# Sparse attention: queries and values projected ahead of the key rotation, and its low weight parts all made by GpSimd

## The chip, the core and the metric

One core of a Trainium2 chip runs the whole program in one launch. The metric is the device time of one execution in microseconds (us); less is better. In the views PE is TensorE (PEld its weight loads), DVE VectorE, ACT ScalarE, POOL GpSimd and SP the engine that issues the DMAs.

## What is computed

Two blocks over 512 tokens of width 1024, in float32. The first is a gated linear attention, a short convolution and a sliding-window attention, merged, with a gated feed-forward part behind. The second has two layers, and the change lies in each of them:

```python
for l in range(DEPTH_2):
    h = rmsnorm_2(x, norm_mix[l])
    proj = h @ w_in[l]
    aq, ak, av, iq, ik, iw, hq, hf, hi, hg, ga, gb = jnp.split(proj, split_points, axis=-1)
    aq = apply_rope(rmsnorm_2(aq.reshape(B, T, ATTN_HEADS, ATTN_HEAD_DIM), q_norm[l]), cos, sin)
    ak = apply_rope(rmsnorm_2(ak.reshape(B, T, ATTN_HEADS, ATTN_HEAD_DIM), k_norm[l]), cos, sin)
    ...
    y_attn = dsa_attention(aq, ak, av, iq, ik, iw)
```

`dsa_attention` scores every query against every earlier key with four small index heads, takes the 128 best keys of each query, and does the softmax of eight heads of width 64 over these alone. A gated recurrence (HGRN2) runs beside it; both are merged, and a feed-forward part ends the layer.

## The kernel before, in words

One Tile program: a scheduler gives each engine a queue, and each engine works through its queue in order. The scheduler follows the order in which the program is written, and a model of its own of when operations can run; `high_priority` sections (weight loads, evictions) go ahead of what is written before them.

**Weights.** Each float32 weight is used as a sum of a high and a low part, so that a product is three matmuls. `weights()` (L133 to L154) has SP load a block into `wraw` (three buffers); ACT casts the high part `whi` (L149), and an engine taken in turn from the list `self.lows` subtracts it to make the low part `wlo` (L152). `mixing()` (L101) sets that list to POOL, POOL, DVE; `feeding()` (L104) to DVE alone. There are three buffers of `whi` and of `wlo` each.

**Projections.** `project_tokens` (L156) gives tokens on partitions: for each of eight weight blocks and four groups of 128 tokens the matmuls L168 (`wlo`), L169 and L170, so 12 matmuls for each low part and 96 for a projection. `project` (L184) gives features on partitions, with L193 to L195.

**The sparse attention** is `dsa()` (L820), called by `second_mix` (L949). Its steps stand in the order of the string ORDER (L25): `x` projects the index inputs, `h` the gated values of the recurrence, `X` rotates the index inputs. `1`, `2`, `3` select the keys of the second to fourth group of 128 queries (over 256, 384 and 512 keys): sixteen rounds on DVE of a maximum (L878) and a replacement (L879), closed by L880. The first group needs no selection. `k`, `q`, `v` project keys, queries and values; for keys and queries ACT squares the result and DVE sums it (L805). `K` and `Q` rotate: `rotated()` (L810) makes a reciprocal root from those sums on DVE (L229 to L233), and for each of four groups of tokens `rope()` (L785) multiplies by the cosine table on POOL (L791) and by the sine table in two halves on DVE (L792, L793) and adds both on POOL (L794); then DVE scales by the root (L817) and PE transposes (L239). `a` to `d` attend, one group of queries each: scores on PE (L917), mask and maximum on DVE (L919), exponential on ACT (L921), transposes and products on PE (L925, L929). The projections of the recurrence and its heads, written behind `dsa()`, fill PE between these.

```python
        for c in ORDER:
            if c in steps:
                steps[c]()
            elif c in "123":
                select(int(c))
            else:
                attend("abcd".index(c))
```

Of the kernel before, what the change touches and what calls it, by code (L numbers as in the profile page):

```python
# [21 lines left out]
KD = 8  # L22
KF = 22
WARM = 12
ORDER = "xhX123kKqvQabcd"  # L25
EPS = 1e-6
NEG = -1e30
UNSEEN = -2e38
# [42 lines left out]
class Builder:  # L71
# [748 lines left out]
    def dsa(self, l, X):  # L820
# [62 lines left out]
        def inputs(j, name):  # L883
            got[name] = self.attention_inputs(A["w_tok"][l, j], X, name)
# [21 lines left out]
        def attend(i):  # L906
# [28 lines left out]
            for m in range(4):  # L935
# [3 lines left out]
                     q=lambda: inputs(1, "aq"), Q=rotate_queries, v=values, h=gated_values)  # L939
        for c in ORDER:  # L940
            if c in steps:
# [7 lines left out]
    def second_mix(self, l, X):  # L949
        nc, A = self.nc, self.A  # L950
        W = A["w_in2"][l]
        it = iter(range(W.shape[0]))
        proj = lambda: self.project(W[next(it)], X)

        with self.on("a"):
            yattn = self.dsa(l, X)
        if self.pending:
            self.settle()
        hv = self.hv
        yh = []  # L960
        for hd in range(4):
            F = self.scaled(proj(), "hf", self.i)
            k = self.i("hk")
            nc.scalar.activation(k, F, AF.Sigmoid, scale=-1.0)
            nc.scalar.activation(F, F, AF.Sigmoid)
            if l:
                nc.gpsimd.tensor_scalar(k, k, self.om[:, hd:hd + 1], None, op0=OP.mult)
                nc.vector.tensor_scalar(F, F, self.om[:, hd:hd + 1], self.lb[:, hd:hd + 1], op0=OP.mult, op1=OP.add)
            q = self.silu2(proj(), "hq")
            v = [a[:, hd * P:(hd + 1) * P] for a in hv]  # L970
            g = self.silu2(proj(), "hg")
            yh.append(self.hgrn_head(F, q, k, v, g, self.half[:, 4 + l:5 + l], "yh"))

        acc = self.merge(A["w_gate2"][l, 0], X, A["w_po"][l, 0], yattn, None, 2, False)
        return self.merge(A["w_gate2"][l, 1], X, A["w_po"][l, 1], yh, acc, 4, True)
# [121 lines left out]
```

## Time and profile before

| | us |
|---|---|
| three runs | 2609.94, 2606.26, 2607.33 |
| their median | 2607.33 |
| span of the profiled execution (no other time is given for it) | 2605.2 |
| PE busy | 2533.9 (97%) |
| DVE busy | 1355.5 (52%) |
| ACT busy | 1000.8 (38%) |
| POOL busy | 754.3 (29%) |

The span runs from the first to the last instruction of the profiled execution; it lies 0.08% below the median of the runs. Busy shares are means over the whole program. A timeline row gives start, duration, engine, line, operation, result and inputs, and in brackets the time that the engine was idle before it and the instruction that ended the wait. PEclk is the clock granted to TensorE as a share of the full 2.4 GHz; 0.50 is the lower level of 1.2 GHz.

### The profile page before, as it was taken

The numbers are of one execution on the slowest core, as the hardware profiler recorded it, in microseconds if no ns is written. First come the engines' busy times: TensorE is split into PE (matmuls) and PEld (weight loads), VectorE is DVE, ScalarE is ACT, GpSimd is POOL, SyncE is SP. The second block draws the span as 40 slices with busy tenths as digits, with TensorE's granted clock in tenths as the row PEclk, the third lists the DMA queues.
The fourth block names the chain that finished last, engine by engine and source line by source line (L and its number), as shares of the span: only waits on it lengthen the run. The fifth ranks groups of instructions, "written<-read, shape, count | busy, mean of one in ns | idle before, by whom it ended". The sixth has DMA issues, their size and how long they took to land.

```text
span 2605.2 us, 31523 instructions
## 1 busy us (share of the span) xinstructions
PE 2533.9 (97%) x11742; PEld 2040.0 (78%) x11742; DVE 1355.5 (52%) x2568; ACT 1000.8 (38%) x1813; POOL 754.3 (29%) x640
## 2 busy tenths in 40 slices
PE   9999999999999997999999999999799999999999
PEld 7777888788888865777878888887577787888887
DVE  4565322477774579675244444336967524444432
ACT  5543333444443333553343333334354433433321
POOL 4234334511101234443351111013545435211100
PEclk9999999999999999999999999999899999999999
DMA  3112222222222221111322222322110122222232
GB/s 135 57 51 81 93 94 93 101 97 96 97 94 90 90 73 65 42 41 51 99 96 94 97 95 94 96 88 81 65 49 33 45 94 97 97 97 97 95 101 87
DMA packets 67434, 217.66 MB, mean 84 GB/s; under 512 B 7744, under 2 KB 8640, under 8 KB 67280
## 3 DMA queue, kind: packets, MB, share of 16 engines
q1 hardware_dynamic: 67280, 215.65, 24.9%
q8 instruction: 92, 1.51, 0.2%
q14 instruction: 62, 0.51, 0.1%
HBM read 213.52 MB, written 2.10 MB: 83 GB/s over the span
## 4 chain that ended last, share of the span: by engine, by line
PE 83%; DVE 12%; issue 2%; POOL 2%; ACT 1%; DMA 0%; SPq 0%; DVEq 0%; POOLq 0%; ACTq 0%
PE mm L194 24%; PE mm L195 24%; PE mm L193 24%; PE at L917 1%; PE mm L169 1%; PE mm L168 1%; PE mm L170 1%; DVE score L879 1%; PE at L929 1%; DVE m L878 1%; DVE wlo L152 1%; PE at L239 1%; DVE hf L490 1%; DVE rope L792 1%; DVE rsq_w L232 1%
## 5 line engine op out<-in xcount | busy, mean ns | idle before, releaser
L149 ACT CAST whi<-wraw 128x512 fp32r<-128x512 f32 (+3 forms) x824 | 502.2, 610 | 1177.7 <-PE mm L195 992.1
L194 PE MATMUL mm<-xl,whi 128*128 128x512 f32 x1920 | 757.2, 394 | 0.0
L193 PE MATMUL mm<-xh,wlo 128*128 128x512 f32 x1920 | 756.8, 394 | 0.0
L195 PE MATMUL mm<-xh,whi 128*128 128x512 f32 x1920 | 755.5, 393 | 0.0
L152 DVE TENSOR_TENSOR wlo<-wraw,whi 128x512 fp32r<-128x512 f32 (+1 forms) x529 | 387.4, 732 | 457.9 <-ACT whi L149 455.2
L152 POOL TENSOR_TENSOR wlo<-wraw,whi 128x512 fp32r<-128x512 f32 (+2 forms) x295 | 383.6, 1301 | 767.0 <-ACT whi L149 747.1
L194 PEld LDWEIGHTS mm<-xl,whi 128*128 128x128 f32 x1920 | 361.7, 188 | 79.8 <-issue 7.5
L195 PEld LDWEIGHTS mm<-xh,whi 128*128 128x128 f32 x1920 | 361.6, 188 | 78.2 <-issue 5.6
L193 PEld LDWEIGHTS mm<-xh,wlo 128*128 128x128 f32 x1920 | 361.5, 188 | 76.6 <-issue 3.5
L193 PE MATMUL mm<-acth,wlo 128*128 128x512 f32 x528 | 208.6, 395 | 0.0
L195 PE MATMUL mm<-acth,whi 128*128 128x512 f32 x528 | 208.6, 395 | 0.0
L194 PE MATMUL mm<-actl,whi 128*128 128x512 f32 x528 | 208.6, 395 | 0.0
L725 POOL TENSOR_TENSOR fg<-fg,rstd 128x512 f32<-128x512 f32 x44 | 56.7, 1289 | 426.1 <-ACT fg L724 426.1
L168 PE MATMUL mm<-wlo,xh 128*128 128x512 f32 (+2 forms) x384 | 146.6, 382 | 20.0 <-POOL wlo L152 12.4
L170 PE MATMUL mm<-whi,xh 128*128 128x512 f32 (+2 forms) x384 | 144.5, 378 | 0.0
L169 PE MATMUL mm<-whi,xl 128*128 128x512 f32 (+2 forms) x384 | 144.2, 375 | 0.2 <-DVE xl L281 0.2
L202 DVE TENSOR_TENSOR gate<-mm,rstd 128x512 f32<-128x512 f32 x56 | 38.7, 691 | 169.3 <-PE mm L195 169.3
L270 POOL TENSOR_TENSOR acc<-acc,sq 128x512 f32<-128x512 f32 x39 | 58.7, 1506 | 205.9 <-ACT sq L267 204.9
L195 PEld LDWEIGHTS mm<-acth,whi 128*128 128x128 f32 x528 | 99.0, 187 | 24.3
L193 PEld LDWEIGHTS mm<-acth,wlo 128*128 128x128 f32 x528 | 99.0, 187 | 24.2
L194 PEld LDWEIGHTS mm<-actl,whi 128*128 128x128 f32 x528 | 99.0, 187 | 24.2
L168 PEld LDWEIGHTS mm<-wlo,xh 128*128 128x128 f32 x384 | 73.5, 191 | 40.7 <-POOL wlo L152 15.7
(347 smaller groups left out, 3288.3 us busy)
## 6 DMA issues: line engine op xcount, KB each, us to landing
wraw<-in_w_ffn_in SPq DMA_DIRECT2D x88, 512.0 KB, 3.2
wraw<-in_w_gate SPq DMA_DIRECT2D x56, 512.0 KB, 3.2
wraw<-in_w_in SPq DMA_DIRECT2D x52, 512.0 KB, 3.2
wraw<-in_w_up SPq DMA_DIRECT2D x44, 512.0 KB, 3.2
wraw<-in_w_tok SPq DMA_DIRECT2D x32, 512.0 KB, 3.2
wraw<-in_w_ffn_out SPq DMA_DIRECT2D x32, 512.0 KB, 3.5
wraw<-in_w_down SPq DMA_DIRECT2D x16, 512.0 KB, 3.5
wraw<-in_w_po SPq DMA_DIRECT2D x32, 256.0 KB, 2.6
```

The costliest lines, as they stand in the source:

```text
L149: nc.scalar.copy(wh, raw[:, k:k + m, :])
L152: eng.tensor_tensor(wl, raw[:, k:k + m, :], wh.bitcast(F32), op=OP.subtract)
L168: nc.tensor.matmul(ps[t][:, 0:w], xh, wl, start=i == 0, stop=False)
L169: nc.tensor.matmul(ps[t][:, 0:w], xl, wh, start=False, stop=False)
L170: nc.tensor.matmul(ps[t][:, 0:w], xh, wh, start=False, stop=i == KD - 1)
L193: nc.tensor.matmul(ps, wl, xh, start=i == 0, stop=False)
L194: nc.tensor.matmul(ps, wh, xl, start=False, stop=False)
L195: nc.tensor.matmul(ps, wh, xh, start=False, stop=i == n - 1)
L202: self.nc.vector.tensor_tensor(out, ps, other, op=OP.mult)
L232: nc.vector.scalar_tensor_tensor(w, w, -0.5, y, op0=OP.mult, op1=OP.mult)
L270: (nc.vector if d % 2 and len(acc) > 1 else nc.gpsimd).tensor_tensor(a, a, sq, op=OP.add)
L725: nc.gpsimd.tensor_tensor(g, g, self.rstd, op=OP.mult)
```

## The change

The steps `q` and `v` move ahead of `K`, and while `dsa()` is written down, `self.lows` holds POOL alone, so that every low part there is POOL's; behind it the list of three is set again.

```diff
-ORDER = "xhX123kKqvQabcd"
+ORDER = "xhX123kqvKQabcd"
...
         with self.on("a"):
+            self.lows = [nc.gpsimd]
             yattn = self.dsa(l, X)
+            self.mixing()
```

How this moves instructions in the second layer of the second block (the first reads alike from its key projection on). In the names, `akx` and `aqx` are keys and queries, `tabC` and `tabS` their tables of cosine and sine, `rope` the two products, `aro` the rotated tile, `m` the eight maxima.

POOL from the selection on, before:

```order
L152 TENSOR_TENSOR wlo<-wraw,whi 128x512 x11
L791 TENSOR_TENSOR rope_14688<-akx,tabC 128x512
L152 TENSOR_TENSOR wlo<-wraw,whi 128x512
L794 TENSOR_TENSOR aro<-rope_14688,rope_14689 128x512
L791 TENSOR_TENSOR rope_14705<-akx,tabC 128x512
L794 TENSOR_TENSOR aro<-rope_14705,rope_14706 128x512
L152 TENSOR_TENSOR wlo<-wraw,whi 128x512
L791 TENSOR_TENSOR rope_14722<-akx,tabC 128x512
```

and now:

```order
L152 TENSOR_TENSOR wlo<-wraw,whi 128x512 x24
L791 TENSOR_TENSOR rope_14997<-akx,tabC 128x512
L152 TENSOR_TENSOR wlo<-wraw,whi 128x512
L794 TENSOR_TENSOR aro<-rope_14997,rope_14998 128x512
L152 TENSOR_TENSOR wlo<-wraw,whi 128x512
L791 TENSOR_TENSOR rope_15014<-akx,tabC 128x512
L152 TENSOR_TENSOR wlo<-wraw,whi 128x512
L794 TENSOR_TENSOR aro<-rope_15014,rope_15015 128x512
L791 TENSOR_TENSOR rope_15031<-akx,tabC 128x512
L152 TENSOR_TENSOR wlo<-wraw,whi 128x512
L794 TENSOR_TENSOR aro<-rope_15031,rope_15032 128x512
L791 TENSOR_TENSOR rope_15048<-akx,tabC 128x512
```

24 low parts now stand ahead of the first key rotation, and between the adds L794 of keys and queries stand 4, 3, 3, 3, 3, 2 and 2 operations of POOL, the add itself counted.

DVE at the first key rotation, before, among the rounds over 384 keys:

```order
L793 TENSOR_TENSOR rope_14689<-akx,tabS 128x8x32
L879 MATCH_REPLACE score<-m_14413,score 128x384
L231 TENSOR_TENSOR rsq_w<-akss,rsq_y 128x32
L878 MAX m_14416<-score 128x8
L232 SCALAR_TENSOR_TENSOR rsq_w<-rsq_w,rsq_y 128x32
L792 TENSOR_TENSOR rope_14706<-akx,tabS 128x8x32
```

and now, among the rounds over 512 keys:

```order
L805 TENSOR_REDUCE aqss<-asq 128x8 x2
L879 MATCH_REPLACE score<-m_14484,score 128x512
L792 TENSOR_TENSOR rope_14998<-akx,tabS 128x8x32
L878 MAX m_14487<-score 128x8
L793 TENSOR_TENSOR rope_14998<-akx,tabS 128x8x32
L879 MATCH_REPLACE score<-m_14487,score 128x512
L812 TENSOR_SCALAR aqss<-aqss 128x32
L817 TENSOR_TENSOR aro<-aro,rsq_y 128x512
L878 MAX m_14490<-score 128x8
L792 TENSOR_TENSOR rope_15015<-akx,tabS 128x8x32
```

The first key rotation stands behind nine rounds over 512 keys and all four sums of the queries, and no low part stands in this stretch.

PE around the last key transposes and the query transposes, now (the first row's eight are the first two groups of keys):

```order
L239 MATMUL at<-csts,aro 128x128 x8
L193 MATMUL mm<-xh,wlo 128x512
L194 MATMUL mm<-xl,whi 128x512
L195 MATMUL mm<-xh,whi 128x512
L193 MATMUL mm<-xh,wlo 128x512
L194 MATMUL mm<-xl,whi 128x512
L239 MATMUL at<-csts,aro 128x128 x4
L195 MATMUL mm<-xh,whi 128x512
L239 MATMUL at<-csts,aro 128x128 x4
L193 MATMUL mm<-xh,wlo 128x512
L239 MATMUL at<-csts,aro 128x128 x4
L194 MATMUL mm<-xl,whi 128x512
```

Ahead of these eight transposes stand now all matmuls of the queries and values; before, only those of the keys and the first of the queries did. 13 matmuls of the recurrence's projections stand ahead of the last query transposes, where 5 stood.

## Rows read from the trace of the kernel before

**Rows 1.** Part 1 of the page: busy us, share of the span, instructions.

```profile
PE 2533.9 (97%) x11742; PEld 2040.0 (78%) x11742; DVE 1355.5 (52%) x2568; ACT 1000.8 (38%) x1813; POOL 754.3 (29%) x640
```

**Rows 2.** PE's timeline, second layer's attention: start, us, engine, line, operation [idle before <-releaser].

```profile
1846.85 1.11 PE L239 MATMUL at<-csts,aro 128*128 128x128 f32 x4 [8.25 <-DVE aro L817]
...
1890.27 0.40 PE L195 MATMUL mm<-xh,whi 128*128 128x512 f32 x1
...
1890.50 0.39 PE L193 MATMUL mm<-xh,wlo 128*128 128x512 f32 x1
...
1893.00 0.33 PE L925 MATMUL at<-csts,aL 128*128 128x128 f32 x1 [0.75 <-ACT aL L921]
```

**Rows 3.** Windows: us, busy of PE, PEld, DVE, ACT, POOL, PEclk, DMA share, GB/s.

```profile
1798.00:1845.00 47.00, 37.82 (x158) 28.98 (x157) 46.03 (x118) 14.88 (x25) 21.10 (x17) 0.93 0.19 68
...
1845.00:1888.20 43.20, 36.63 (x158) 28.86 (x158) 41.02 (x85) 18.69 (x42) 21.84 (x17) 0.92 0.22 73
...
1842.00:1846.00 4.00, 0.00 (x0) 0.00 (x0) 4.00 (x9) 0.00 (x0) 2.41 (x3) 0.50 0.00 0
...
1850.00:1854.00 4.00, 4.00 (x19) 3.29 (x19) 3.97 (x11) 2.83 (x13) 1.03 (x1) 0.75 0.00 0
```

**Rows 4.** DVE: low parts by window (busy, count), then groups by form, 1790 to 1893.

```profile
1795.00:1888.00 93.00, 7.25 (x7) 0.93 0.20 68
...
1798.00:1852.28 54.28, 3.78 (x4) 0.87 0.20 68
...
L792 DVE TENSOR_TENSOR rope<-akx,tabS 128x256 f32<-128x256 f32 x4 | 2.8, 698 | 0.0
...
L793 DVE TENSOR_TENSOR rope<-akx,tabS 128x256 f32<-128x256 f32 x4 | 1.6, 412 | 0.0
...
L231 DVE TENSOR_TENSOR rsq_w<-akss,rsq_y 128x32 f32<-128x32 f32 x3 | 3.1, 1036 | 0.0
```

**Rows 5.** DVE's timeline in the same stretch.

```profile
1840.97 1.75 DVE L152 TENSOR_TENSOR wlo<-wraw,whi 128x512 fp32r<-128x512 f32 x1
...
1852.28 0.35 DVE L880 TENSOR_SCALAR score<-score 128x384 f32<-128x384 f32 x1
...
1856.10 0.69 DVE L152 TENSOR_TENSOR wlo<-wraw,whi 128x512 fp32r<-128x512 f32 x1 [2.08 <-ACT whi L149]
...
1887.44 0.67 DVE L817 TENSOR_TENSOR aro<-aro,rsq_y 128x512 f32<-128x512 f32 x1
...
1888.04 0.68 DVE L878 MAX8 m<-score 128x8 f32<-128x512 f32 x1
...
1889.54 0.69 DVE L878 MAX8 m<-score 128x8 f32<-128x512 f32 x1
```

**Rows 6.** POOL's timeline: the adds of the key rotation, then of the query rotation.

```profile
1830.29 1.29 POOL L794 TENSOR_TENSOR aro<-rope,rope 128x512 f32<-128x512 f32 x1 [1.99 <-DVE rope L793]
...
1834.34 1.28 POOL L794 TENSOR_TENSOR aro<-rope,rope 128x512 f32<-128x512 f32 x1 [1.49 <-DVE rope L793]
...
1839.41 1.26 POOL L794 TENSOR_TENSOR aro<-rope,rope 128x512 f32<-128x512 f32 x1 [1.32 <-DVE rope L793]
...
1843.76 1.26 POOL L794 TENSOR_TENSOR aro<-rope,rope 128x512 f32<-128x512 f32 x1 [1.59 <-DVE rope L793]
...
1865.29 1.29 POOL L794 TENSOR_TENSOR aro<-rope,rope 128x512 f32<-128x512 f32 x1 [0.52 <-DVE rope L793]
...
1870.36 1.29 POOL L794 TENSOR_TENSOR aro<-rope,rope 128x512 f32<-128x512 f32 x1 [0.53 <-DVE rope L793]
...
1873.71 1.29 POOL L794 TENSOR_TENSOR aro<-rope,rope 128x512 f32<-128x512 f32 x1 [0.53 <-DVE rope L793]
...
1878.93 1.27 POOL L794 TENSOR_TENSOR aro<-rope,rope 128x512 f32<-128x512 f32 x1 [1.46 <-DVE rope L793]
```

**Rows 7.** PE's timeline, first layer, projection of the gated values: two waits.

```profile
917.82 0.50 PE L168 MATMUL mm<-wlo,xh 128*128 128x512 f32 x1 [2.31 <-POOL wlo L152]
...
921.97 0.50 PE L168 MATMUL mm<-wlo,xh 128*128 128x512 f32 x1 [1.13 <-DVE wlo L152]
```
## The prediction

> **What bounds the kernel now.** The page's first part comes first: TensorE (PE) is busy 2533.9 of 2605.2 us [rows 1]. The change touches only the two sparse attentions, so next I read PE's timeline there, where the bracket gives the idle time before an instruction and who ended it. In the second layer the largest hole is 8.25 us ahead of the first key transposes at 1846.85, which wait for DVE's last step of the key rotation (L817); then come waits for low parts, for query transposes, and 0.75 us ahead of the first attention transpose (L925) at 1893.00 [rows 2]. From about 1770 to 1893 these sum to some 20 us; the first layer repeats them 855.1 us earlier. The windows say why: DVE is busy 46.03 of 47.00 and 41.02 of 43.20 us, POOL about half [rows 3]. So the stage ends when one chain ends on DVE: sixteen rounds of maximum and replacement for each of three row blocks, with rotations and low parts between them. The profiled time is the span, 2605.2; the median of the three runs is 2.1 above it (0.08%). I add the sum to the median.
>
> **What moves.** No matmul, DMA or cast is added or taken away, and SP issues the same loads of the same size, with the loads of queries and values before the key transposes where keys' and queries' loads stood before. The order on the engines (the change's section) shows three moves.
>
> *1. Low parts leave DVE.* In 1798 to 1888 DVE makes seven, 7.25 us in all, four of them (3.78) before 1852.28 [rows 4]. All go to POOL at about 1.3 us each; POOL made its 16 beside other work.
>
> *2. The rotation of the keys leaves the select rounds of the 384-wide block,* and goes behind nine of the sixteen rounds of the 512-wide block. What leaves ahead of the 384-wide block's end (L880, 1852.28) is four low parts 3.78, four L792 2.8, four L793 1.6 and four L817 about 3.35, together 11.5; successive DVE rows overlap by 0.07, which over these sixteen is 1.1; and the small steps of the root wait less for POOL (L231 took 1036 ns on 32 columns), for which I estimate 1.6 [rows 4, 5]. So 12.0 us go, and the block ends at 1840.3. Then eight more rounds than before stand ahead of the first key rotation, at 1.50 each (1888.04 to 1889.54) [rows 5], 12.0 in all; four reductions (L805), an estimated 2.4 from the 0.67 of the similar full-width L817 row; and L792, a maximum and L793, 1.3. First key L793 ends at 1840.3 + 15.7 = 1856.0, and POOL's add (L794) starts there; before it started at 1830.29 [rows 6].
>
> *3. POOL now makes low parts between the rotation's own operations.* What POOL's rows show is a ping-pong: POOL multiplies, DVE does L793, POOL adds, DVE scales (L817). From one L794 to the next it took 4.05, 5.07 and 4.35 us for the keys and 5.07, 3.35, 5.22 for the queries; the short ones hold two POOL operations (mean 3.9), the long ones three (mean 5.1) [rows 6]. In the new order the seven intervals hold 4, 3, 3, 3, 3, 2 and 2. That is 5.1 + 1.3 for the four, 4 x 5.1, 2 x 3.9: 34.6; two L817 and a low part stand on DVE ahead of the third query's rotation, 1.4 more: 36.0. The last L794 starts at 1892.0, is 1.3 long, and with 0.15 of handing over and L817's 0.65 the last query is scaled at 1894.1; before it was at 1888.11 [rows 5]. **The rotation ends 6.0 us later.**
>
> **What this does to PE.** The 8.25 hole goes from where it was: 192 matmuls of queries and values stand ahead of it now. But values' last four low parts stand behind the key adds on POOL, which leaves PE waiting an estimated 3.3, 0.6, 2.3 and 2.2 us, then some 8 for the first query and 5 for the others: 19 to 22 idle against some 16 over the same matmuls. I don't add these; the end counts. From the last L817's end to L925 it was 1893.00 - 1888.11 = 4.9; the 0.75 of wait there goes, since all select rounds are over by then, so L925 comes at 1894.1 + 4.15 = 1898.25, 5.25 later. Ahead of it stand 8 more projection matmuls (24 against 16), which needn't be done later: 8 x 0.23 (1890.27 to 1890.50 [rows 2]) = 1.8. Net **+3.4 a layer**. Both new holes of 4 and 8 us may lower PE's clock: in 1842 to 1846 it stood at 0.50, in 1850 to 1854 at 0.75, after the hole of 8.25 [rows 3]. At half rate eleven matmuls cost 2.5 more; since one such hole exists before too, I take 0.5, with 0 and 2.5 as ends.
>
> At the first layer's start the third low part of the gated values falls behind one more index rotation on POOL. PE waited 2.31 for it until 917.82; the next wait, 1.13 at 921.97 for DVE, goes [rows 7]. Net an estimated 1.0. The second layer keeps its order there.
>
> **Sum:** 1.0 + 2 x (3.4 + 0.5) = +8.8: 2607.3 + 8.8 = **2616**.
>
> *Bounds of the ping-pong,* which no row shows in this mix: below, POOL never waits and its 20 operations take 1.29 each, 25.8 in place of 36.0, so 10.2 less, -6.8 a layer. Above, 39 (the four-operation pattern at 5.1 + 1.3 in three more places would give 39.9) with 2.5 of clock: +3.4 + 3 + 2.5, about +9 a layer. I take 36 since the nearest rows, with the same operations on the same engines, lie at 3.35 to 5.22 each and none at POOL's bare speed. The stage breaks even at 36.0 - 3.4 = 32.6.
>
> **The rivals.**
>
> *Faster: DVE is the only bound.* Then the chain just loses seven low parts; one comes back ahead of the third query (+0.7), three select rounds that ended after the rotation now end before it (+4.5), and the 2.08 us that DVE idled before a low part at 1856.10 [rows 5] go. -7.25 + 0.7 + 4.5 - 2.1 = -4.1; with 1.8 for the matmuls and 0.75 for the wait -6.7 a layer, and 1.0 at the start: 2607.3 - 12.4 = **2595** (own range 2592 to 2602). For it speaks DVE's 46.03 of 47.00 [rows 3]; against it, that the rotations now run in one row at the end, where POOL's 20 operations decide. It decides if the seven intervals sum to some 26 us.
>
> The Trainium skill, "Perfetto Trace Analysis", section "Optimizing Scalar/DVE Operations", says that with a saturated DVE some work may go to Scalar or even GPSIMD, but that moving work between GPSIMD and DVE might not help, since they share an SBUF read port. The first half would give the 2595 of this rival; the second speaks for the forecast. This trace shows the sharing: DVE's low part took 1.75 us at 1840.97 while POOL ran, against 0.69 at 1856.10 [rows 5].
>
> *No change: the ping-pong sums to 31 to 34.* Holes move from keys to values and queries, with the same sum, and the end stays: 2602 to 2612.
>
> *The change doesn't do what it says.* The order rows exclude it: no low part stays on DVE in the stretch but one at its end, and PE's first key transposes stand behind the values.
>
> **How the numbers follow.** About 0.2% (5.2 us) is what a measurement of this kernel can tell from no change: faster is below 2602.1, slower above 2612.5. Forecast 0.54, no change 0.26, faster rival 0.20. The forecast's own range, 2608 to 2626, begins within 0.2%: 0.08 of it counts as same. Of the no-change case 0.02 lie beyond each side. So faster 0.20 + 0.02 = 0.22, same 0.08 + 0.22 = 0.30, slower 0.46 + 0.02 = 0.48. The range 2598 to 2626 leaves out half of the faster case and the tail above.
>
> **What would show it.** Right: in the second layer PE's hole before the keys' transposes is no longer the first; PE waits for POOL's low parts of the values instead; the first key L794 starts near 1856; the seven intervals sum to about 36; L925 comes near 1898. Wrong: if L794's intervals are under 4.6 in the mean, POOL's low parts slip into its waits for DVE and cost nothing, and the faster rival holds; if DVE idles in the rotation, it is POOL that bounds; if PE's clock stays at 0.50 for long after the holes, the upper end holds.

## The result, and the profile after

| | before | changed |
|---|---|---|
| median of the runs | 2607.44 us (4 runs) | 2633.37 us (4 runs, 2632.66 to 2634.96) |
| ratio | | 1.0099, 95% interval 1.0084 to 1.0113 |
| span of the profiled execution | 2605.2 us | 2633.2 us |

The changed kernel is 25.9 us slower. The profiled execution, at 2634.96, lies 1.6 above its median; of the 28.0 us between the spans 2.0 have already come up where the first attention's projections begin (first L168 at 888.5 in place of 886.5), in code that the change leaves alone, and no part of what follows.

The first part of the page of the changed kernel, answering to [rows 1]:

```profile
PE 2541.7 (97%) x11742; PEld 2047.0 (78%) x11742; DVE 1351.9 (51%) x2540; ACT 1006.3 (38%) x1817; POOL 792.7 (30%) x668
```

PE has the same 11742 matmuls and 7.8 us more busy time; the other 20 us are idle time. To see where, I cut each layer at events that both traces have: the first matmul of the index projection (L168), the first matmul of the selection's scores (L867), the first transpose of the attending (L925) and the start of the last accumulation of the merge (L684, DVE). I call the pieces start, rotation and rest. The view of one line gives the first and the last start; second layer of the changed kernel:

```profile
L867 PE MATMUL at<-ikT,iqT x24: 376/534/693, 1807.9 to 1816.2; 64*128 64x256 f32 x8, 64*128 64x384 f32 x8, 64*128 64x512 f32 x8
...
L925 PE MATMUL at<-csts,aL x80: 270/273/418, 1915.7 to 2085.9; 128*128 128x128 f32 x80
...
L684 DVE TENSOR_TENSOR acc<-acc,gate x4: 1085/1110/1148, 2212.4 to 2221.8; 128x512 f32<-128x512 f32 x4
```

and of the kernel before:

```profile
L867 PE MATMUL at<-ikT,iqT x24: 376/534/693, 1791.3 to 1799.7; 64*128 64x256 f32 x8, 64*128 64x384 f32 x8, 64*128 64x512 f32 x8
...
L925 PE MATMUL at<-csts,aL x80: 270/272/329, 1893.0 to 2057.9; 128*128 128x128 f32 x80
...
L684 DVE TENSOR_TENSOR acc<-acc,gate x4: 1086/1110/1149, 2184.5 to 2193.9; 128x512 f32<-128x512 f32 x4
```

So the rotation (first L867 to first L925) took 101.7 us before and 107.8 now, and the rest (to the last L684) went from 300.9 to 306.1. All six pieces:

| changed less before, us | first layer | second layer | forecast for each |
|---|---|---|---|
| start | +2.8 | +0.9 | +1.0 and 0 |
| rotation | +6.2 | +6.2 | +5.25, and 0.5 for the clock |
| rest | +4.6 | +5.3 | -1.8 (eight matmuls done earlier) |

The pieces sum to 26.0, the forecast to 8.8. The rotation is nearly as forecast; the rest is off by 6.4 and 7.1.

**The rotation.** POOL's adds L794 in the second layer, answering to [rows 6]:

```profile
1874.09 1.26 POOL L794 TENSOR_TENSOR aro<-rope,rope 128x512 f32<-128x512 f32 x1 [8.43 <-DVE rope L793]
...
1880.11 1.28 POOL L794 TENSOR_TENSOR aro<-rope,rope 128x512 f32<-128x512 f32 x1 [0.42 <-DVE rope L793]
...
1884.95 1.29 POOL L794 TENSOR_TENSOR aro<-rope,rope 128x512 f32<-128x512 f32 x1 [0.43 <-DVE rope L793]
...
1889.78 1.29 POOL L794 TENSOR_TENSOR aro<-rope,rope 128x512 f32<-128x512 f32 x1 [0.42 <-DVE rope L793]
...
1895.57 1.28 POOL L794 TENSOR_TENSOR aro<-rope,rope 128x512 f32<-128x512 f32 x1 [1.56 <-DVE rope L793]
...
1900.38 1.28 POOL L794 TENSOR_TENSOR aro<-rope,rope 128x512 f32<-128x512 f32 x1 [0.55 <-DVE rsq_w L232]
...
1905.90 1.31 POOL L794 TENSOR_TENSOR aro<-rope,rope 128x512 f32<-128x512 f32 x1 [3.02 <-DVE rope L793]
...
1909.46 1.27 POOL L794 TENSOR_TENSOR aro<-rope,rope 128x512 f32<-128x512 f32 x1 [1.03 <-DVE rope L793]
```

From the first to the last of them it is 35.4 us; the walk had 36.0. The first stands 66.2 us after the first L867; in the time of before (L867 at 1791.3) that is 1857.5, where the walk had 1856.0. PE's holes there, answering to the 8.25 of [rows 2]:

```profile
1876.63 0.79 PE L168 MATMUL mm<-wlo,xh 128*128 128x512 f32 x1 [6.03 <-POOL wlo L152]
...
1889.41 0.50 PE L168 MATMUL mm<-wlo,xh 128*128 128x512 f32 x1 [1.82 <-POOL wlo L152]
...
1904.03 1.09 PE L239 MATMUL at<-csts,aro 128*128 128x128 f32 x4 [7.20 <-DVE aro L817]
...
1909.12 1.08 PE L239 MATMUL at<-csts,aro 128*128 128x128 f32 x4 [2.73 <-DVE aro L817]
```

The hole ahead of the key transposes is gone, and PE waits 6.03 and 1.82 for the values' low parts and 7.20 and 2.73 for scaled queries instead. Windows of 4 us (columns as in [rows 3]) show what the holes do to the clock:

```profile
1878.00:1882.00 4.00, 4.00 (x12) 3.09 (x11) 4.00 (x8) 0.06 (x1) 3.58 (x4) 0.57 0.30 98
...
1902.00:1906.00 4.00, 1.97 (x9) 1.82 (x9) 3.93 (x8) 0.59 (x1) 0.98 (x2) 0.50 0.11 46
```

The granted clock stood near or at its lower level of 1.2 GHz after the two long ones, where before it did so behind one hole [rows 3].

DVE lost its low parts there, and the rotation still ended later. Groups by form in the rotation, changed kernel:

```profile
L817 DVE TENSOR_TENSOR aro<-aro,rsq_y 128x512 f32<-128x512 f32 x8 | 9.5, 1199 | 2.6 <-POOL aro L794 2.6
...
L880 DVE TENSOR_SCALAR score<-score 128x512 f32<-128x512 f32 x1 | 1.5, 1487 | 0.0
```

and before:

```profile
L817 DVE TENSOR_TENSOR aro<-aro,rsq_y 128x512 f32<-128x512 f32 x8 | 6.0, 754 | 0.0
...
L880 DVE TENSOR_SCALAR score<-score 128x512 f32<-128x512 f32 x1 | 0.4, 428 | 0.0
```

The eight scalings L817 take 1199 ns each in place of 754, 3.5 us in all, and the closing step over 512 columns 1487 in place of 428. The scalings that stand beside an operation of POOL are the long ones: five of the eight now, at 1.11 to 1.77 us, against 0.68 to 0.69 for the other three; before, one of the eight did (1.33). It is mostly the new order that brings them there: without the attention's low parts (below) they still take 1128. On top of that all sixteen rounds over 512 keys now stand ahead of the last scaling, where three came after it.

**The rest.** Whole windows of it, before and changed, second layer (columns as in [rows 3]):

```profile
1893.00:2193.90 300.90, 296.65 (x1527) 234.46 (x1528) 159.09 (x345) 124.48 (x245) 129.83 (x126) 1.00 0.19 64
...
1915.70:2221.80 306.10, 297.26 (x1519) 233.88 (x1518) 161.35 (x342) 126.90 (x246) 129.56 (x125) 0.99 0.19 62
```

PE's idle time grows from 4.25 to 8.84 us, and its busy time by 0.6, though it has eight matmuls fewer. In the first layer it is 4.3 us more idle time and 0.2 more busy time. In both layers the granted clock was at its lower level once, for 3.4 us (from 1942.8 in the second).

PE's groups from the first to the last transposed head of the attending, second layer, changed kernel (behind the second bar the idle time before the group and who ended it):

```profile
L502 PE MATMUL at<-lvx 128*126 128x64 f32 (+4 forms) x160 | 20.2, 269 | 2.8 <-DVE lvx L486 1.4 <-DVE AT L504 1.2
...
L239 PE MATMUL at<-csts,hG 128*128 128x128 f32 x16 | 2.8, 287 | 2.4 <-POOL hG L508 2.4
...
L239 PE MATMUL at<-csts,ron 128*128 128x128 f32 x12 | 2.0, 286 | 1.6 <-DVE ron L408 1.6
...
L481 PE MATMUL at<-lvx,ones 128*128 128x256 f32 x8 | 2.8, 428 | 0.7 <-POOL lvx L479 0.7
```

and before:

```profile
L502 PE MATMUL at<-lvx 128*126 128x64 f32 (+4 forms) x160 | 19.8, 262 | 1.4 <-DVE lvx L486 1.4
...
L239 PE MATMUL at<-csts,hG 128*128 128x128 f32 x16 | 2.7, 283 | 0.1
...
L239 PE MATMUL at<-csts,ron 128*128 128x128 f32 x12 | 1.9, 277 | 0.0
...
L481 PE MATMUL at<-lvx,ones 128*128 128x256 f32 x8 | 2.8, 429 | 0.1
```

New are 2.4 us of waiting for POOL's last product of the recurrence's heads (L508), 1.6 for their normalised output and 1.2 for DVE's L504. None of these instructions is in the diff. What differs is the order of the queues, and in it what PE has to do between two of them. PE and, as the last row, POOL at the second recurrence head, changed kernel:

```profile
1986.69 0.65 PE L457 MATMUL at<-lvx 128*64 128x64 f32 x8 [0.27 <-DVE lvx L486]
...
1988.66 0.66 PE L239 MATMUL at<-csts,hG 128*128 128x128 f32 x4 [1.32 <-POOL hG L508]
...
1987.10 1.50 POOL L508 TENSOR_TENSOR hG<-hG,hk 128x512 f32<-128x512 f32 x1
```

and before:

```profile
1968.02 0.68 PE L457 MATMUL at<-lvx 128*64 128x64 f32 x8
...
1968.63 0.50 PE L195 MATMUL mm<-xh,whi 128*128 128x512 f32 x1
...
1968.97 0.39 PE L193 MATMUL mm<-xh,wlo 128*128 128x512 f32 x1
...
1969.19 0.40 PE L194 MATMUL mm<-xl,whi 128*128 128x512 f32 x1
...
1969.43 0.40 PE L195 MATMUL mm<-xh,whi 128*128 128x512 f32 x1
...
1969.66 0.38 PE L239 MATMUL at<-csts,hG 128*128 128x128 f32 x2
...
1967.89 1.52 POOL L508 TENSOR_TENSOR hG<-hG,hk 128x512 f32<-128x512 f32 x1
```

In the order of before, four matmuls of a projection stand between L457 and the transposes that need L508's result: L508 ends at 1969.41, and the transposes start at 1969.66 without a wait. In the order of now none stands between: PE is through with L457 at 1987.34, L508 ends at 1988.60, and PE has waited 1.32 us. L508 itself also starts later against L457, 0.41 us behind its start in place of 0.13 ahead of it. The scheduler has written the stretch behind the attention in another order, although the change says nothing of it. Set side by side, the two traces' rest has some 240 of PE's 1527 instructions in another place in each layer, and some 100 of DVE's 343; POOL's order is all but the same. No run here tells PE's order from DVE's.

### The profile page after: what moved, and what is told of

Read it like the earlier page. It is cut to its first block, busy times and chain, and to the rows that moved or that the text cites. A ratio compares the mean times of both kernels' runs of the same rounds, so it can differ in the third digit from the quotient of the medians.

```text
span 2633.2 us, 31516 instructions
## 1 busy us (share of the span) xinstructions
PE 2541.7 (97%) x11742; PEld 2047.0 (78%) x11742; DVE 1351.9 (51%) x2540; ACT 1006.3 (38%) x1817; POOL 792.7 (30%) x668
## 4 chain that ended last, share of the span: by engine, by line
PE 80%; DVE 14%; POOL 3%; issue 2%; ACT 1%; DMA 0%; SPq 0%; POOLq 0%; DVEq 0%; ACTq 0%
PE mm L194 23%; PE mm L195 23%; PE mm L193 23%; DVE score L879 2%; DVE m L878 2%; PE at L917 1%; PE at L929 1%; PE mm L168 1%; PE at L239 1%; PE mm L169 1%; DVE rsq_w L231 1%; PE mm L170 1%; POOL hG L488 1%; DVE aro L817 1%; DVE acc L684 1%
## 5 line engine op out<-in xcount | busy, mean ns | idle before, releaser
L152 POOL TENSOR_TENSOR wlo<-wraw,whi 128x512 fp32r<-128x512 f32 (+2 forms) x323 | 418.0, 1295 | 751.6 <-ACT whi L149 732.0
L152 DVE TENSOR_TENSOR wlo<-wraw,whi 128x512 fp32r<-128x512 f32 (+1 forms) x501 | 363.6, 726 | 417.3 <-ACT whi L149 414.7
L168 PE MATMUL mm<-wlo,xh 128*128 128x512 f32 (+2 forms) x384 | 147.3, 383 | 31.0 <-POOL wlo L152 24.3
L168 PEld LDWEIGHTS mm<-wlo,xh 128*128 128x128 f32 x384 | 74.1, 193 | 51.0 <-POOL wlo L152 28.6
```

Of the source, the lines that this page charges most:

```text
L152: eng.tensor_tensor(wl, raw[:, k:k + m, :], wh.bitcast(F32), op=OP.subtract)
L168: nc.tensor.matmul(ps[t][:, 0:w], xh, wl, start=i == 0, stop=False)
```

## Experiments

For each run: its edit, what was expected, and what came. Each is against the kernel before on the same chip, 2607.5 to 2608.2 us there. The expectations speak of the attending, which ends with the last L929; what was measured is given for the whole rest, to the last L684, since matmuls that leave the attending come back behind it.

### The two halves apart

The order of the steps alone:

```diff
-ORDER = "xhX123kKqvQabcd"
+ORDER = "xhX123kqvKQabcd"
```

> Only the order of the steps changes (queries and values ahead of the key rotation); the low parts go POOL, POOL, DVE as before. Theory A (the order costs: both rotations run in one row at the end of the selection, and the attending behind them gets fewer projection matmuls to fill its holes): 16 to 24 us slower than before, of it some 5 us a layer between the first L867 and the first L925 and some 4 us a layer between the first L925 and the last L929. Theory B (the low parts on POOL cost, by stretching the exchange of POOL and DVE): within 6 us of before, attending as long as before.

The low parts alone:

```diff
+            self.lows = [nc.gpsimd]
             yattn = self.dsa(l, X)
+            self.mixing()
```

> Only the low parts change (all on POOL in the sparse attention); the order is that of before. Theory A: 3 to 9 us slower, of it 3 to 4 at the two starts (index inputs and gated values) and little else; attending as long as before (166 us a layer). Theory B: 14 to 22 us slower, with the L794 adds further apart and L925 5 us or more later in each layer.

Measured: the order alone 2628.18 us (ratio 1.0080, 1.0067 to 1.0094), the low parts alone 2626.90 (1.0074, 1.0062 to 1.0087). Neither theory holds as put: the first run came in size and pieces as theory A has it and the second in size as B has it, but each half costs some 20 us, and both together only 25.9. The pieces say why. The order alone brings the rotation's loss (+5.1 and +5.9); the low parts alone have the rotation at +0.7 and +1.3, not the 5 or more of theory B; but **both** lengthen the rest, by 3.2 and 3.6 us (with 12 matmuls done earlier, worth 2.7) and by 6.9 and 7.3 us. The rest's loss is something that either half sets off, and that can't be had twice.

### The start

```diff
         for c in ORDER:
+            if c in "xh":
+                self.lows = [nc.gpsimd]
+            else:
+                self.mixing()
```

> Order of before; POOL makes all low parts only for the index inputs and the gated values, the rest as before. If the loss at the two starts (2.8 and 1.0 us in the profile of the changed kernel) is the low parts', some 3 to 4 us slower; if those were chance, 0 to 1.

Measured: 2615.32 us (1.0028, 1.0016 to 1.0039), 7.9 slower, twice what was expected. The starts are 4.3 and 2.4 us longer, the rotation 0.4 and 1.4, the rest 0.3 and -0.1. So the loss at the start is that of the low parts, and it is larger than the changed kernel's profile shows: its waits are the same (5.6 us for POOL in the first layer against 5.5), but the clock stood at its lower level behind them for 6.8 us against 3.4, and in the second layer for 3.4 against none. Two more builds with POOL's low parts there have +4.3 in the first layer. PE's queue behind the attention is that of before in this build, and the rest is too.

### The values' low parts on DVE, in the changed kernel

```diff
             if c in steps:
+                self.lows = [nc.vector if c == "v" else nc.gpsimd]
                 steps[c]()
```

> The changed kernel, but the values' eight low parts a layer are made by DVE. If POOL's low parts between the rotation's own operations set its pace, the seven intervals of L794 fall from 35.4 us to some 28 to 30, PE's waits for the values' low parts shrink, and the kernel is 6 to 14 us faster than the changed one. If DVE sets the pace (selection rounds and rotation in one queue), the intervals stay within 2 us, and the kernel is within 4 us of the changed one or slower.

Measured: 2632.43 us, 0.9 below the changed kernel: the second answer. The seven intervals sum to 37.8 us, not less than 35.4, though POOL has three low parts between them in place of six. DVE got the values' low parts instead, so the run speaks for DVE's queue and does not yet say what POOL's low parts are worth; that comes below.

### What sets off the loss in the rest

Only the values' low parts on POOL, the order of before (`mixing()` for all other steps; no step is in the empty string); then the same with the keys' in place of the values':

```diff
             if c in steps:
+                if c in "v":
+                    self.lows = [nc.gpsimd]
+                elif c in "":
+                    self.lows = [nc.vector]
+                else:
+                    self.mixing()
                 steps[c]()
+                self.mixing()
```

> Order of before; only the values' eight low parts a layer are all POOL's. PE's queue up to the first L925 reads as before, and behind it as in the changed kernel. Theory C (the loss in the attending is the order that the scheduler gives PE behind the first L925, where transposes of the recurrence stand right behind the matmuls they depend on): the attending is 4 to 7 us a layer longer, with 2.4 us of waits for POOL's L508 as in the changed kernel, the rotation within 2 us of before, in all 8 to 16 us slower. Theory D (the attending is longer because the rotation ends later and has eaten matmuls that filled its holes): attending within 1 us of before, in all 0 to 4 us slower.

> Order of before; only the keys' eight low parts a layer are all POOL's. PE's queue behind the first L925 is that of before but for a row or two. Theory C: attending within 1 us of before. Any difference then is the rotation's: if low parts off DVE bring the key rotation forward, 1 to 5 us faster; if POOL's longer queue gives that back, within 2 us of before. Theory D: attending moves with the end of the rotation, in its direction.

The keys projected ahead of the third selection:

```diff
-ORDER = "xhX123kKqvQabcd"
+ORDER = "xhX12k3KqvQabcd"
```

> Low parts as before; the keys are projected ahead of the third selection, and rotated behind its scores, so that 66 matmuls of the queries stand ahead of the first key transposes and 14, 11 and 16 between them, in place of 3 or fewer. PE's queue behind the first L925 is that of before. If DVE's one chain sets the end of the query rotation whatever PE does in between, the hole at the key transposes shrinks by 6 us or more but L925 comes within 2 us of before, and the time with it; if the hole itself costs, 4 to 12 us faster over both layers. Attending within 1 us of before by theory C.

The changed kernel with the turn of the list moved on:

```diff
             self.lows = [nc.gpsimd]
             yattn = self.dsa(l, X)
             self.mixing()
+            self.count += 2
```

> The changed kernel, with the turn of the list of three moved on by two behind the attention, so that other low parts of the recurrence's weights are DVE's; the scheduler then arranges PE's queue behind the first L925 in a third way, while the rotation stays as in the changed kernel. Theory C: the attending differs from the changed kernel's by 2 us or more a layer, either way, with other waits in it; the rotation stays within 1 us. Theory D: attending within 1.5 us of the changed kernel's.

Measured: with the values' low parts on POOL 2630.02 us (1.0077, 1.0063 to 1.0090). The rotation is 1.2 and 0.2 us longer, the rest 7.0 and 14.0. That is theory C's case, though more than the 8 to 16 us it gave: nothing moved ahead of L925 on PE, no matmul was done earlier, and the loss is there, with the waits of the changed kernel. PE's groups in the second layer's attending, and one wait:

```profile
L239 PE MATMUL at<-csts,hG 128*128 128x128 f32 x16 | 2.8, 287 | 2.4 <-POOL hG L508 2.4
...
L239 PE MATMUL at<-csts,ron 128*128 128x128 f32 x12 | 2.0, 286 | 1.6 <-DVE ron L408 1.6
...
1981.45 0.66 PE L239 MATMUL at<-csts,hG 128*128 128x128 f32 x4 [1.33 <-POOL hG L508]
```

Two windows, 1976 to 1980 and 1984 to 1988, around that wait:

```profile
1976.00:1980.00 4.00, 3.74 (x33) 3.14 (x32) 3.57 (x10) 0.97 (x3) 3.61 (x6) 1.00 0.37 133
...
1984.00:1988.00 4.00, 4.00 (x15) 3.13 (x14) 2.15 (x8) 1.22 (x5) 0.00 (x0) 0.50 0.01 4
```

A wait of 1.33 us, and the granted clock, 1.00 ahead of it, is 0.50 in the window after: here the wait cost more than its length. It need not: behind the like wait of the changed kernel, 1.32 us until 1988.66, the clock stayed up:

```profile
1988.00:1992.00 4.00, 3.34 (x22) 2.56 (x23) 3.32 (x9) 1.60 (x4) 0.60 (x1) 1.00 0.02 4
```

The second layer's 14.0 hold two stretches at the lower clock (the other behind a wait of 2.8 us for ACT, just ahead of its first L925), 17.1 us in all, the first layer's 7.0 one of 3.4. An estimate from half speed puts them at 8.5 and 1.7 us, which leaves 5.5 and 5.3. The profiled execution is the longest of four that lie between 2625.9 and 2631.3.

With the keys' low parts on POOL 2611.18 us (1.0012, 1.0003 to 1.0021): rest -0.1 and -0.2, rotation +0.6 and +1.5, the whole 2.9 slower, outside both answers. PE's queue behind the attention is that of before, and nothing is lost there; nothing is won in the rotation either, by low parts off DVE.

With the keys ahead of the third selection 2609.15 us (1.0004, 0.9996 to 1.0013), rest 0.0 and 0.3. PE's holes in the second layer:

```profile
1842.45 0.80 PE L168 MATMUL mm<-wlo,xh 128*128 128x512 f32 x1 [2.67 <-DVE wlo L152]
...
1849.96 1.11 PE L239 MATMUL at<-csts,aro 128*128 128x128 f32 x4 [5.86 <-DVE aro L817]
...
1894.15 0.33 PE L925 MATMUL at<-csts,aL 128*128 128x128 f32 x1 [0.82 <-ACT aL L921]
```

The hole ahead of the key transposes shrinks from 8.25 to 5.86 (6 or more was expected to go), and a new one of 2.67 us for a low part stands ahead of it. L925 comes 101.7 us after L867, as before. The idle time was moved more than filled: 5.86 and 2.67 make 8.53. That the end of the query rotation on DVE decides, whatever PE does in between, fits this; what closing the hole would be worth isn't shown.

With the turn moved on 2636.54 us (1.0108, 1.0092 to 1.0123): the rest is 5.1 and 3.8 us longer than before, so within 1.5 of the changed kernel's, though its largest wait is another one (POOL's L479, 3 us). Of the expectation, the other waits came, the difference of 2 us a layer didn't, and the rotation, which was to stay, is 2.3 and 1.1 us longer than in the changed kernel: this run tells C from D no further.

### Without any low part

These two runs leave out the low parts in the sparse attention: the matmuls read the high part in their place. (The low parts of the recurrence's weights stay; two of them are made by POOL between the adds.)

```diff
-                eng.tensor_tensor(wl, raw[:, k:k + m, :], wh.bitcast(F32), op=OP.subtract)
+                if self.skip:
+                    wl = wh
+                else:
+                    eng.tensor_tensor(wl, raw[:, k:k + m, :], wh.bitcast(F32), op=OP.subtract)
...
+            self.skip = True
             yattn = self.dsa(l, X)
+            self.skip = False
```

> Order of before, and in the sparse attention no low part is computed at all: the matmuls read the high part in its place, as many as before. The rotation (first L867 to first L925) without any low part on DVE or POOL: by the forecast's faster rival (DVE's chain just loses them) 6 to 8 us shorter a layer; if most of DVE's low parts fit in time it loses otherwise, 0 to 3 us shorter.

> Order of the change, no low part computed in the sparse attention, else as the run before it. The order's own price in the rotation is the difference of the two: if the low parts on POOL stretch the exchange (the forecast's walk), the seven intervals fall from 35.4 to some 27 us (seven of 3.9) and L925 comes 6 to 9 us earlier than in the changed kernel; if DVE's own queue sets the pace, by less than 4 us.

Measured: 2606.43 us with the order of before (1.0002, 0.9993 to 1.0011) and 2606.76 with the order of the change (0.9995, 0.9986 to 1.0004). In the order of before the rotation is 4.3 and 2.8 us shorter: between the two answers in the first layer, inside the lower one in the second, and well under the 7.25 us that DVE no longer spends on low parts. In the order of the change L925 comes 5.8 and 6.4 us earlier than in the changed kernel. But the line view of the adds (L798 in this kernel), second layer, shows where this does not come from:

```profile
L798 POOL TENSOR_TENSOR aro<-rope,rope x8: 1263/1285/1310, 1844.2 to 1877.2; 128x512 f32<-128x512 f32 x8
```

From the first to the last it is 33.0 us, against 35.4 with four more low parts on POOL between them, and 27 in the expectation. Most of the gain, 4.8 us, comes ahead of the exchange (the first add stands 61.4 us after L867 in place of 66.2), where DVE's operations run beside a quieter POOL: the steps that close the selection over 256 and 384 columns take 282 and 351 ns there, 1016 and 943 in the changed kernel. In both runs the rest is longer (7.5 and 8.9; 3.6 and 7.5): these builds, too, have another order there than the kernel before.

### A product of the recurrence on DVE

```diff
-        nc.gpsimd.tensor_tensor(G, G, k, op=OP.mult)
+        nc.vector.tensor_tensor(G, G, k, op=OP.mult)
```

In the changed kernel:

> The changed kernel, with the recurrence's last product (L508), for which PE waited 2.4 us a layer in the attending, on DVE in place of POOL; PE's queue behind the first L925 then stands half way between that of before and of the changed kernel. If those waits are the loss, the attending is 2 to 4 us a layer shorter than in the changed kernel and the whole 4 to 8 us faster than it; if other waits take their place, within 3 us of the changed kernel.

In the kernel with the values' low parts on POOL:

> Order of before, the values' low parts on POOL, and L508 on DVE; PE's queue up to the first L925 is that of before, behind it half way between the two arrangements. If the wait for POOL's L508 and what follows from it carry the loss of the attending, it is 4 to 8 us a layer shorter than with the values' low parts on POOL alone (+7.0 and +14.0 there), and the kernel within 5 us of before; if other waits take its place, within 3 us of that kernel.

Measured: 2624.14 us (1.0064, 1.0052 to 1.0077), 16.3 slower than before in place of 25.9, more of a gain than the 4 to 8 expected; the rest goes from +4.6 and +5.3 to -1.5 and +0.6, the rotation stays (+6.9, +6.3). In the other, 2615.35 (1.0029, 1.0020 to 1.0039), 7.6 slower in place of 21.8, where within 5 was expected: the rest goes from +7.0 and +14.0 to +2.1 and +2.6. PE's groups there, second layer:

```profile
L239 PE MATMUL at<-csts,hG 128*128 128x128 f32 x16 | 2.5, 280 | 0.0
...
L239 PE MATMUL at<-csts,ron 128*128 128x128 f32 x12 | 2.1, 287 | 1.0 <-DVE ron L408 1.0
```

The wait for L508 is gone (2.4 to 0.0) and that for the normalised output fell from 1.6 to 1.0. The move also changed the order of PE's queue, which now stands between the two, and the second layer was at the lower clock for 3.4 us in place of 17.1; so this is the wait, the order and the clock together, not the wait alone.

### A faster version

The gated values' low parts on DVE, then the same with L508 on DVE:

```diff
             if c in steps:
+                if c in "":
+                    self.lows = [nc.gpsimd]
+                elif c in "h":
+                    self.lows = [nc.vector]
+                else:
+                    self.mixing()
                 steps[c]()
+                self.mixing()
```

> Order of before; the gated values' eight low parts a layer are all DVE's, so that none stands on POOL behind the index rotation. PE's queue behind the first L925 is that of before. If the waits at the start (2.3 to 2.6 us a layer for POOL's low part, 1.1 for DVE's in the first) are the place on POOL, the starts become 2 to 4 us shorter in each layer and the kernel 3 to 8 us faster than before; if DVE, which has its halves of the rotation there, brings the wait back, within 2 us of before.

> Order of before, the gated values' low parts on DVE, and L508 on DVE; PE's queue behind the first L925 is that of before but for a row or two. As PE waits only 0.2 us for L508 in that arrangement, moving it should give little: the starts 1 to 2 us a layer shorter as with the gated values alone, the attending within 1 us of before, in all 2 to 6 us faster than before.

Measured: **2603.85 us** (0.9983, 0.9974 to 0.9992), 4.0 faster than before, the only version here that beats both. The starts are 1.3 and 2.2 us shorter, rotation and rest within 0.2. PE's waits for low parts at the second layer's start (the second row is under the heading of idle time):

```profile
L168 PE MATMUL mm<-wlo,xh x67: 309/389/496, 1743.7 to 1786.9; 128*128 128x512 f32 x35, 128*128 128x324 f32 x32
...
  DVE wlo L152: 0.4, 1
```

Before, PE waited 2.6 us for POOL in this place, the like of the first wait of [rows 7]; now it is 0.4 for DVE. With L508 on DVE as well, 2606.35 (0.9992, 0.9984 to 1.0001): no gain, as expected of L508, but the gain at the start is given back by rotation (+1.6, +1.8) and by the rest of the second layer (+2.5), where PE's queue has another order again; in the first layer it is that of before but for a few rows, and the rest is 0.8 shorter.

### All pieces

Differences from before in us, first and second layer; matmuls are the projection matmuls of the recurrence that come ahead of L925 beyond those of before, 0.23 us each.

| | start | rotation | rest | matmuls | median |
|---|---|---|---|---|---|
| changed kernel | +2.8, +0.9 | +6.2, +6.2 | +4.6, +5.3 | 8 | +25.9 |
| order alone | 0.0, +1.7 | +5.1, +5.9 | +3.2, +3.6 | 12 | +20.7 |
| low parts alone | +2.8, +0.8 | +0.7, +1.3 | +6.9, +7.3 | 0 | +19.4 |
| POOL for index and gated values | +4.3, +2.4 | +0.4, +1.4 | +0.3, -0.1 | 0 | +7.9 |
| POOL for values | 0.0, +1.7 | +1.2, +0.2 | +7.0, +14.0 | 0 | +21.8 |
| POOL for keys | 0.0, +0.4 | +0.6, +1.5 | -0.1, -0.2 | 1 | +2.9 |
| keys ahead of the third selection | 0.0, +0.1 | +0.5, 0.0 | 0.0, +0.3 | 0 | +0.9 |
| changed, values on DVE | +2.9, +0.9 | +11.3, +11.1 | -0.2, -0.8 | 28 | +25.0 |
| changed, turn moved on | +4.3, +2.5 | +8.5, +7.2 | +5.1, +3.8 | 5 | +28.3 |
| changed, L508 on DVE | +4.3, +0.9 | +6.9, +6.3 | -1.5, +0.6 | 8 | +16.3 |
| POOL for values, L508 on DVE | 0.0, +1.9 | +0.5, +1.3 | +2.1, +2.6 | 0 | +7.6 |
| gated values on DVE | -1.3, -2.2 | +0.1, +0.2 | +0.1, 0.0 | 0 | -4.0 |
| gated values and L508 on DVE | -2.9, -2.3 | +1.6, +1.8 | -0.8, +2.5 | 0 | -1.4 |
| no low part, order of before | -6.5, -4.2 | -4.3, -2.8 | +7.5, +8.9 | 0 | -1.5 |
| no low part, order of the change | -6.5, -4.2 | +0.4, -0.3 | +3.6, +7.5 | 8 | -1.1 |

A single cell can be off by the clock alone: with the order alone and with POOL for the values nothing changes at the start and PE is idle there as long as before (3.7 us for 3.8), yet the second start is 1.7 longer, at a mean granted clock of 0.96 in place of 1.00.

Put the matmuls back (8 x 0.23 and so on), and the rest's loss is 6.5 and 7.1 in the changed kernel, 5.9 and 6.3 with the order alone, 6.9 and 7.3 with the low parts alone, 6.3 and 5.6 with the values on DVE: much the same, whatever the rotation does. In all builds that have another order there and leave L508 on POOL it lies between 4.9 and 9.3, but for the 14.0 above. It is 0.3 or less in the four builds whose queues behind the attention, PE's and DVE's, are those of before but for a few rows (POOL for index and gated values, POOL for keys, keys ahead of the third selection, gated values on DVE).

## Why the prediction was wrong

The direction was right, the size was not: +8.8 was forecast, +25.9 measured, outside the range. Of the 17 us between them 13.5 are the rest's, 2.7 the start's and 0.9 the rotation's.

**The step that failed** is the one on what lies behind L925: "Ahead of it stand 8 more projection matmuls (24 against 16), which needn't be done later: ... 1.8". The matmuls were done earlier as counted. But the sentence takes the program behind L925 as unchanged, and it was not: the scheduler had put PE's transposes of the recurrence right behind the matmuls that they follow, and they waited for POOL and DVE. With the eight matmuls put back that cost 6.5 and 7.1 us a layer: 4.3 and 4.6 us of more idle time (in the second layer the new waits of 2.4, 1.6 and 1.2, less some that went), and 2.1 and 2.4 of longer matmuls, of which the 3.4 us at the lower clock are worth an estimated 1.7. That the loss goes with the changed order is shown by the builds above; how much of it is PE's order and how much DVE's is not. The prediction followed the two orders up to L925 and no further. Carried on behind it, the comparison shows the changed queue before anything has run; its price could have been estimated from the rows of before, where POOL's L508 ends 0.25 us ahead of the transposes that need it.

**The start** was mis-sized: 1.0 was forecast, 3.7 came. Waits for low parts rose in the first layer from 4.1 (3.0 for POOL, 1.1 for DVE) to 5.5, and the clock fell behind the longest of them, 3.69 us, which it had not done before; the second layer, put at nothing, has 0.9 (waits of 3.1 for 2.6). The run with POOL for the index and gated values alone shows that this is the low parts'.

**The rotation** came out as walked (first add 1857.5 for 1856.0, intervals 35.4 for 36.0, L925 6.2 us later for 5.25), but half of its reason was wrong. I had put five of the seven intervals at three or four POOL operations, so that POOL's low parts cost some 8 of the 36 us. Without the attention's low parts the intervals still sum to 33.0, so that these are worth 2.4 there, and with the values' on DVE to 37.8. The order alone already makes the rotation 5.1 and 5.9 us longer. DVE's queue, rounds and rotation in one row, sets the pace: over the 35.4 us DVE is busy 33.9, POOL 27.9. That the walk's sum came out so near was in part luck.

**The faster rival** (DVE is the only bound, and just loses seven low parts) fell: with all low parts gone from DVE and the order of before the rotation is 0.7 and 1.3 us longer. Even with no low part in the attention it is only 4.3 and 2.8 shorter, where 7.25 us leave DVE. The Trainium skill, "Perfetto Trace Analysis", section "Optimizing Scalar/DVE Operations", warns that moving work between GPSIMD and DVE might not help because of a shared SBUF read port; the run with the low parts alone agrees with the warning: seven low parts left DVE, and its L817 grew from 754 to 885 ns and its L792 from 698 to some 1260.

**Of the signs** that I named, those for the first hole, the values' low parts, the first add and the intervals came as written; L925 near 1898 too (1899.2 in the time of before). None of them looked behind L925.

What the scheduler goes by when it flips the order behind the attention stays open. The runs show what sets it off (the values' low parts on POOL, the rotations behind the values, or no low parts at all) and what doesn't (POOL for the keys' low parts, or for the index's and the gated values').

## What to carry to other kernels

Where a scheduler orders the queues, an edit's price is not confined to the code it touches: compare the orders of the whole program, not only up to the point where the edit ends, and look there for an instruction that now comes before its input from another engine is ready. A hole in the busiest engine need not be worth its length while another engine's chain sets the end; here each new order moved the hole, and none closed it, so that this last is argued and not shown. And work taken from a saturated VectorE to GpSimd can be given back: here VectorE's own operations grew beside it.

## What was not expected of the hardware

- With POOL for the values, a wait of TensorE of 1.33 us was followed by a window at the lower clock (0.50, after 1.00); the 6.8 us at half speed that the second layer of that run had there cost more than the wait. In the changed kernel a wait of 1.32 us at the same place left it at 1.00 (1988 to 1992), and there a wait of 0.95 us, until 1941.85, was followed by 3.4 us at the lower level. So the length of the one wait doesn't decide. In the kernel before, waits of up to 0.98 us in the same part left the clock at 1.00.
- A DVE operation over 512 columns in SBUF took 428 ns beside a quiet POOL and 1487 ns where POOL ran a rotation's product and a low part back to back (L880); the eight-maxima instructions of the selection did not change (683 and 686 ns, L878 over 512 columns). The Trainium skill, "SBUF — State Buffer", section "SBUF: two separate sides", says that some DVE operations and a GpSimd operation shut each other out of a shared port pair for a whole instruction; L880 and L817 agree, and what the rows add is the size.
